# 320 dense tokens and 224 gathered slots in the expert stage, with all gate matrices made on TensorE

## The chip, the cores and the metric

The kernel runs on one core of one Trainium2 chip. The metric is the device time of one execution in microseconds (us); lower is better. The engines are TensorE (PE; its weight loads are listed as PEld), VectorE (DVE), ScalarE (ACT), GpSimd (POOL) and SyncE (SP). SP, ACT and POOL also issue DMAs.

## What is computed

One layer over 512 prompt tokens and 32 sample tokens, width 1024, all in float32. A mixer (gated attention with 8 heads of 64 beside a linear recurrence of width 512) is followed by a layer norm, and then by PEER, a retrieval over 16384 single-neuron experts:

```python
def peer_block(xb, w_query, keys_1, keys_2, u_tab, v_tab):
    qy = (xb @ w_query).reshape(n, 8, 2, 128)
    s1 = einsum("nhd,kd->nhk", qy[:, :, 0], keys_1)      # 128 keys per half
    s2 = einsum("nhd,kd->nhk", qy[:, :, 1], keys_2)
    t1, i1 = top_k(s1, 16); t2, i2 = top_k(s2, 16)
    cand = t1[..., :, None] + t2[..., None, :]           # 256 pairs
    top, sel = top_k(cand, 16); g = softmax(top)
    idx = take_along_axis(i1 * 128 + i2, sel)            # 8 heads x 16 experts of a token
    act = gelu(einsum("nhkd,nd->nhk", u_tab[idx], xb))
    return einsum("nhk,nhkd->nd", g * act, v_tab[idx])   # then residual and layer norm
```

## The kernel before

**Precision.** A float32 product is made of three TensorE passes: each operand is split into a rounded high part (a copy on ACT) and a low part (a subtraction), and `mm3` adds high*high, low*high and high*low. So every 128x1024 weight tile costs one DMA of 512 KB, one ACT copy and one subtraction (`split`, L112 to L119; `table` in the expert stage, L1146 to L1154). `pool_share` says which share of the subtractions of `split` goes to POOL; the others go to DVE.

**Stages.** `run` works in two groups of tokens: group 0 is the sample S (32) with prompt tiles P0 and P1 (128 each), group 1 is P2 and P3. The order is mixer(0), `out_first` (output projection, layer norm and PEER queries of group 0), mixer(1), `out_second` (the same for group 1), `experts`.

**Background.** Each `chunk` (24 matmuls over one weight tile) ends with `background`, which issues pieces from the list `bg` at a set rate (`MIX_RATE`, `OUT_RATE`). The pieces are zero fills of the gate matrix and the steps of `route`: for one head of one token tile, two rankings of 128 scores, a ranking of the candidate pairs, and the pick of indices and softmax weights (`gate`). The framework orders each engine's instructions by a modelled timeline, near the order in which they are issued; some are pinned by `keep_in_program_order`.

**Dense and gathered tokens.** For P0, P1 and P2 (384 tokens) all 16384 experts are computed in 128 blocks: `up(b)` (24 matmuls, 384 columns) and a GELU give a 128x384 activation tile, `down(b)` multiplies it with the gates of the block, splits it, and adds it into six PSUM banks with 18 matmuls of 512 columns. The first `down` follows 29 blocks behind `up` (`AHEAD`). For S (packed four times onto 128 partitions: 32 slots) and P3 (128 slots) the chosen rows alone are fetched: for each slot one indirect DMA on POOL's queue brings 128 rows of `peer_u` and another 128 rows of `peer_v` (512 KB each); DVE takes the dot product with h (`u_step`, L1068) and adds the weighted row (`v_step`, L1083). `RATE` gives the fetches per block; 29/10 per block is the usual one. Six buffers (`gat`) hold rows.

**Gates.** For P0 and P1 the gates are scattered into a zeroed matrix in DRAM by 256 indirect DMAs on POOL (`scatter`, L998, 16 per head and tile), each with an add; the 32 zero fills of 512 KB go through SP's queue. Every `down` reads its 128 KB of them (`gt`, L1172) behind all scatters. For P2 `gate_steps` builds 4 tokens at a time: DVE makes one-hot rows, TensorE multiplies them (L1041), ACT copies the result, and a DMA stores 16 tokens (`gatemat2`), which is read back in chunks of 16 blocks (`gg`, L1202).

**Queues near the change.** POOL's stream holds the scatters, the gathers, a memset of two rows of `qa` (L356) in mixer(1), and a share of the subtractions. SP's stream holds all weight loads in order and the two small DMAs of `forget` (L503, L504) into `ka` and `qa`, which attention needs.

## Time and profile before

| | us |
|---|---|
| median of 3 runs | 1828.71 (1826.39 to 1833.19) |
| the profiled execution | 1824.01 |
| its span, first to last instruction | 1822.2 |
| outside the span | 1.8 |
| busy PE, DVE, POOL, ACT | 1677.2, 1398.2, 928.0, 810.2 |
| DMA | 443.01 MB, mean 243 GB/s |

The profile is of one execution. A group of instructions is told by its line, engine and operands; "busy" is the union of its times, and "idle before" is how long its engine stood still just before, with what ended that. PE's instructions overlap, so the pace of matmuls is read from the chain of waits, where pieces follow each other without overlap.

### The profile page before, as it was taken

The numbers are of one execution on the slowest core, as the hardware profiler recorded it, in microseconds if no ns is written. First come the engines' busy times: TensorE is split into PE (matmuls) and PEld (weight loads), VectorE is DVE, ScalarE is ACT, GpSimd is POOL, SyncE is SP. The second block draws the span as 40 slices with busy tenths as digits, with TensorE's granted clock in tenths as the row PEclk, the third lists the DMA queues.
The fourth block names the chain that finished last, engine by engine and source line by source line (L and its number), as shares of the span: only waits on it lengthen the run. The fifth ranks groups of instructions, "written<-read, shape, count | busy, mean of one in ns | idle before, by whom it ended". The sixth has DMA issues, their size and how long they took to land.

```text
span 1822.2 us, 26970 instructions
## 1 busy us (share of the span) xinstructions
PE 1677.2 (92%) x9448; PEld 1511.8 (83%) x9448; DVE 1398.2 (77%) x3197; ACT 810.2 (44%) x1413; POOL 928.0 (51%) x623
## 2 busy tenths in 40 slices
PE   8999999994898999919999999999999999998896
PEld 7889889984687999918999899989999998997674
DVE  6634779884886789809998877877888878886877
ACT  7744455872645674503445333433333333332332
POOL 2110235888888888864443544453544445542340
PEclk9999999997899999959999999999999999999998
DMA  9863636673466656649989889998999888998883
GB/s 319 280 236 101 218 98 171 152 162 59 71 150 143 162 116 174 174 75 360 334 306 322 297 300 328 349 326 321 340 328 343 322 322 321 321 324 281 292 304 125
DMA packets 182201, 443.01 MB, mean 243 GB/s; under 512 B 53624, under 2 KB 80936, under 8 KB 181040
## 3 DMA queue, kind: packets, MB, share of 16 engines
q1 hardware_dynamic: 93568, 265.80, 42.8%
q0 software_dynamic: 82944, 167.94, 31.0%
q10 hardware_dynamic: 5552, 7.54, 1.3%
q8 instruction: 74, 1.21, 0.3%
q14 instruction: 63, 0.52, 0.1%
HBM read 409.80 MB, written 31.36 MB: 242 GB/s over the span
## 4 chain that ended last, share of the span: by engine, by line
PE 61%; DVE 8%; DMA 6%; POOL 5%; issue 3%; ACT 2%; SPq 0%; DVEq 0%; ACTq 0%; POOLq 0%
PE u L161 9%; PE u L164 9%; PE u L165 9%; PE y L164 8%; PE y L165 8%; PE y L161 8%; POOL gatemat L998 5%; PE mm L164 2%; PE mm L165 2%; PE mm L161 2%; DMA gat<-peer_v,idxP 2%; PE y L1041 1%; DMA vr<-peer_v 1%; DVE wl L119 1%; PE x L895 1%
## 5 line engine op out<-in xcount | busy, mean ns | idle before, releaser
L998 POOL DMA_INDIRECT gatemat<-gateP,idxP x256 | 441.8, 1726 | 94.8 <-issue 72.7
L165 PE MATMUL u<-hDh,ul 128*128 128x384 f32 x992 | 336.3, 339 | 41.3 <-DVE ul L1153 41.3
L161 PE MATMUL u<-hDh,uh 128*128 128x384 f32 x992 | 340.3, 343 | 5.9 <-DVE hS L1097 3.5
L164 PE MATMUL u<-hDl,uh 128*128 128x384 f32 x992 | 336.8, 340 | 0.0
L164 PE MATMUL y<-vl,pwh 128*128 128x512 f32 x768 | 303.1, 397 | 8.2 <-DVE vl L1153 8.1
L165 PE MATMUL y<-vh,pwl 128*128 128x512 f32 x768 | 301.8, 397 | 5.6 <-DVE pwl L1186 5.6
L1058 POOL DMA_INDIRECT gat<-peer_u,idxP x128 | 174.5, 1363 | 213.5 <-DVE ul L1153 43.5
L161 PE MATMUL y<-vh,pwh 128*128 128x512 f32 x768 | 276.5, 396 | 5.5 <-ACT vh L1152 5.5
L1058 POOL DMA_INDIRECT gat<-peer_v,idxP x128 | 172.0, 1344 | 210.0 <-DMA ur<-u_chunk 61.9
L1152 ACT CAST vh<-vr 128x1024 fp32r<-128x1024 f32 x128 | 134.2, 1050 | 296.4 <-DVE vl L1153 150.1
L165 PEld LDWEIGHTS u<-hDh,ul 128*128 128x128 f32 x992 | 188.0, 189 | 42.5 <-DVE ul L1153 42.5
L115 ACT CAST wh<-raw 128x1024 fp32r<-128x1024 f32 (+1 forms) x140 | 145.0, 1039 | 156.4 <-PE mm L164 123.4
L1083 DVE SCALAR_TENSOR_TENSOR accP<-gat,actP,accP 128x1024 f32<-128x1024 f32 x127 | 162.9, 1283 | 66.4 <-DMA gat<-peer_v,idxP 66.0
L119 DVE TENSOR_TENSOR wl<-raw,wh 128x1024 fp32r<-128x1024 f32 (+1 forms) x134 | 164.6, 1230 | 57.1 <-ACT wh L115 56.4
L1068 DVE SCALAR_TENSOR_TENSOR gat<-gat,hP 128x1024 f32<-128x1024 f32 x128 | 155.2, 1220 | 68.3 <-DMA gat<-peer_u,idxP 68.0
L161 PEld LDWEIGHTS u<-hDh,uh 128*128 128x128 f32 x992 | 188.2, 190 | 11.9 <-DVE hS L1097 4.4
L164 PEld LDWEIGHTS u<-hDl,uh 128*128 128x128 f32 x992 | 188.3, 190 | 4.2
L1152 ACT CAST uh<-ur 128x1024 fp32r<-128x1024 f32 x124 | 130.1, 1049 | 125.0 <-DMA ur<-u_chunk 56.9
L164 PEld LDWEIGHTS y<-vl,pwh 128*128 128x128 f32 x768 | 145.5, 189 | 42.8 <-DVE vl L1153 12.7
L165 PEld LDWEIGHTS y<-vh,pwl 128*128 128x128 f32 x768 | 145.4, 189 | 39.5 <-DVE pwl L1186 6.2
L161 PEld LDWEIGHTS y<-vh,pwh 128*128 128x128 f32 x768 | 144.8, 189 | 35.9 <-ACT vh L1152 7.3
L1153 DVE TENSOR_TENSOR vl<-vr,vh 128x1024 fp32r<-128x1024 f32 x128 | 155.9, 1218 | 15.7 <-ACT vh L1152 15.7
(367 smaller groups left out, 3438.1 us busy)
## 6 DMA issues: line engine op xcount, KB each, us to landing
vr<-peer_v SPq DMA_DIRECT2D x128, 512.0 KB
ur<-u_chunk SPq DMA_DIRECT2D x124, 512.0 KB
raw<-w_chunk SPq DMA_DIRECT2D x63, 512.0 KB
gatemat<-zero SPq DMA_DIRECT2D x32, 512.0 KB
raw<-w_q SPq DMA_DIRECT2D x32, 512.0 KB
gt<-gatemat SPq DMA_DIRECT2D x128, 128.0 KB
raw<-w_up SPq DMA_DIRECT2D x16, 512.0 KB
raw<-w_out SPq DMA_DIRECT2D x16, 512.0 KB
```

What stands on the lines that cost most here:

```text
L115: nc.scalar.copy(h, src)
L119: eng.tensor_tensor(out=l, in0=src, in1=h.bitcast(F32), op=OP.subtract)
L161: first = nc.tensor.matmul(out, lh, rh, start=start, stop=False)
L164: nc.tensor.matmul(out, lh, rl, start=False, stop=False)
L165: return first, nc.tensor.matmul(out, ll, rh, start=False, stop=stop)
L895: nc.tensor.matmul(ps[:, i], qT[:, t.col:t.col + t.n], self.keysT[:, half], start=True, stop=True)
L998: i = nc.gpsimd.indirect_dma_start(out=self.G, out_offset=bass.IndirectOffsetOnAxis(ap=t.idx[:, j:j + 1], axis=0), in_=t.gate[:, j:j + 1], ...
L1058: i = nc.gpsimd.indirect_dma_start(out=r, out_offset=None, in_=A[table], in_offset=bass.IndirectOffsetOnAxis(ap=t.idx[:, j:j + 1], axis=0))
L1068: nc.vector.scalar_tensor_tensor(out=r, in0=r, scalar=1.0, in1=t.h, op0=OP.mult, op1=OP.mult, accum_out=act[:, j:j + 1])
L1083: nc.vector.scalar_tensor_tensor(out=acc, in0=r, scalar=act[:, j:j + 1], in1=acc, op0=OP.mult, op1=OP.add)
L1152: nc.scalar.copy(h, raw)
L1153: nc.vector.tensor_tensor(out=l, in0=raw, in1=h.bitcast(F32), op=OP.subtract)
```

## The change

Of P0 only the second half (64 tokens) is still dense, so 320 tokens are dense (`ND`), and the first half (P0a: 64 tokens, packed twice, 64 slots) is gathered: 32 + 64 + 128 = 224 slots. One fetch of a slot brings a row of both tables (`peer_uv`, 8 KB per row, 1 MB per slot); three such buffers take the place of six of half the size. The 64 dense tokens of P0 use 2 products instead of 3 in `down`: low and high parts lie side by side in one 128-column weight, and a matmul with a selection matrix sums the two halves at the end.

All gates are built as those of P2 were; scatters, zero fills, `gt` and its wait are gone. The one-hot rows come from two DVE comparisons, the weighting from four ACT multiplications. `gg` is read in chunks of 8 blocks, issued 4 blocks ahead. Routing works on four heads at a time after the rankings. Nothing is routed in `out_first`; S, P0 and P1 are routed, the gates of P0 and P1 built, and the gathers of S (and whatever comes up of P0a) issued as background of mixer(1) (`early_rows`), four pieces per chunk. These early gathers have one row buffer, inside the tile that later holds h transposed (`hD`); `early_end` empties the list before that tile is filled, and h of group 0 goes through DRAM (`hN`).

In mixer(1) two of three `split` subtractions go to POOL, and in `experts` every `v` subtraction but the last four. The memset of `qa` moves to DVE, and four small DMAs of `forget` from SP's to ACT's queue. `AHEAD` is 32.

```diff
-POOL_SHARE = (1, 5), (0, 1)
-MIX_RATE = (6, 5), (3, 2)
+POOL_SHARE = (1, 5), (2, 3)
+MIX_RATE = (6, 5), (4, 1)
+MIX_GATHER = 3, 4
-OUT_RATE = (3, 2), (1, 1)
+OUT_RATE = (3, 2), (2, 1)
+HALF = 64
+ND = 384 - HALF
-         toks=[Tok("S", 0, 32), Tok("P0", 32, 128, 0, 0), Tok("P1", 160, 128, 128, 128)]),
+         toks=[Tok("S", 0, 32), Tok("P0", 32, 128, 0, 0, HALF), Tok("P1", 160, 128, 128 - HALF, 128)]),
-GT, GB = 16, 16
+GT, GB, UN, NB, LAG = 16, 8, 64, 4, 2
-AHEAD = 29
+AHEAD = 32
-NGAT = 6
+NGAT = 3
-GATHER = AHEAD
-RATE = (1, 1), (26, 10), (29, 10), (16, 10)
+GATHER = 27
+RATE = (1, 2), (13, 10), (16, 10), (8, 10)
...
-                (nc.vector if self.first else nc.gpsimd).memset(self.qa[DH:DH + 2], 1.0)
+                nc.vector.memset(self.qa[DH:DH + 2], 1.0)
...
-        nc.sync.dma_start(self.ka[DH:DH + 1, :, p0:p0 + npr], nF)
-        nc.sync.dma_start(self.qa[DH + 1:DH + 2, :, off:], F)
+        nc.scalar.dma_start(self.ka[DH:DH + 1, :, p0:p0 + npr], nF)
+        nc.scalar.dma_start(self.qa[DH + 1:DH + 2, :, off:], F)
...
+    def early_rows(self, toks):
+        nc, keep = self.nc, self.keep
+        S, P0, P1 = toks
+        ring = keep.tile([P, 2 * KD * max(ND, 288)], F32R, tag="hD", name="ring")
...
+        work = self.routing(S)
+        first = len(work)
+        work += self.routing(P0)
...
+            work.append(lambda: self.halve(P0, t))
+            gathered.append(t)
+        work += self.gate_steps(P0, vt, self.bank, nc.gpsimd, hots.append)
+        work += self.routing(P1)
+        work += self.gate_steps(P1, vt, self.bank, nc.gpsimd, hots.append)
+        for t in gathered:
+            self.steps += self.gather_steps(t)
+        self.bg += work[:first]
+        for i, w in enumerate(work[first:]):
+            self.bg.append(w)
+            if (i + 1) * MIX_GATHER[0] // MIX_GATHER[1] > i * MIX_GATHER[0] // MIX_GATHER[1]:
+                self.bg.append(self.early_step)
+        self.bg += [self.early_step] * 60
+
+    def early_step(self):
+        if self.steps and self.steps[0].tok.done:
+            parts = self.steps[0].parts
+            parts.pop(0)()
+            if not parts:
+                self.steps.pop(0)
+
+    def early_end(self):
+        for p in self.bg:
+            if p != self.early_step:
+                p()
+        self.bg = []
+        while self.steps[0].tok is self.early[0] or len(self.steps[0].parts) < 3:
+            self.early_step()
...
             self.project([t3], 1, lambda half, q: wo[q], behind=True)
+            self.early_end()
+            self.hDh, self.hDl = self.wide("hD")
+            for i, x in enumerate((self.hDh, self.hDl)):
+                nc.gpsimd.dma_start(x[:, :, :NDA], self.hN[:, i])
             self.turned([t2], pool, self.hDh[:, :, c], self.hDl[:, :, c])
...
         def make(t0):
...
+            for m, x in ((0, A), (1, B)):
+                nc.vector.tensor_tensor(out=x, in0=self.iotaK[:, None].to_broadcast(sh),
+                                        in1=T[:, m, t0:t0 + 4, None].to_broadcast(sh), op=OP.is_equal)
             for j in range(4):
+                nc.scalar.mul(A[:, j], A[:, j], T[:, 2, t0 + j:t0 + j + 1])
...
+        def fetch(j):
+            r = v[j] = self.row()
+            i = nc.gpsimd.indirect_dma_start(out=r.rearrange("p i d -> p (i d)"), out_offset=None, in_=A["peer_uv"],
                                              in_offset=bass.IndirectOffsetOnAxis(ap=t.idx[:, j:j + 1], axis=0))
         def u_step(j):
+            r, a = v[j], v["act"][:, j:j + 1]
+            nc.vector.scalar_tensor_tensor(out=r[:, 0], in0=r[:, 0], scalar=1.0, in1=t.h, op0=OP.mult, op1=OP.mult,
+                                           accum_out=a)
+            nc.scalar.activation(a, a, GELU)
+            nc.scalar.mul(a, a, t.gate[:, j:j + 1])
...
         def table(ap, name, stage=None):
...
-            nc.vector.tensor_tensor(out=l, in0=raw, in1=h.bitcast(F32), op=OP.subtract)
+            eng = nc.gpsimd if name == "v" and not stage else nc.vector
+            eng.tensor_tensor(out=l, in0=raw, in1=h.bitcast(F32), op=OP.subtract)
...
         def down(b):
-            gt = pool.tile([P, NS], F32, tag="gt", name="gt", bufs=3)
-            i = nc.sync.dma_start(gt, gates[b * P:(b + 1) * P])
-            for s in [i for c in self.scatters.values() for i in c]:
-                tc.add_manual_dep(i.ins, s.ins.name, SYNC, reason="all heads are in")
-            nc.vector.tensor_tensor(out=a[:, :NS], in0=a[:, :NS], in1=gt, op=OP.mult)
-            a2 = a[:, NS:].rearrange("p (q t) -> p q t", t=GT)
-            nc.vector.tensor_tensor(out=a2, in0=a2, in1=gg[b // GB][:, :, b % GB], op=OP.mult)
+            a3 = a.rearrange("p (q t) -> p q t", t=GT)
+            nc.vector.tensor_tensor(out=a3, in0=a3, in1=gg[b // GB][:, :, b % GB], op=OP.mult)
+            pw = pool.tile([P, UN + 2 * ND], F32R, tag="pw", name="pw", bufs=LAST)
...
+                    if t.nd == UN:
+                        first = nc.tensor.matmul(o, pw[:, :P], vh[:, cs], start=start, stop=False)
+                        nc.tensor.matmul(o, pw[:, :P], vl[:, cs], start=False, stop=stop)
+                    else:
+                        first, _ = self.mm3(o, ph[:, ts], pl[:, ts], vh[:, cs], vl[:, cs], start, stop)
```

## Rows read from the trace of the kernel before

**Rows 1.** Busy time by stage: engine busy us (instructions), clock, DMA share, GB/s.
```profile
core 0: us, PE busy (x) PEld busy (x) DVE busy (x) ACT busy (x) POOL busy (x), PEclk, DMA share, GB/s
0.00:262.00 262.00, 246.21 (x1596) 219.58 (x1597) 154.05 (x336) 143.53 (x249) 42.99 (x44) 0.97 0.65 215
...
322.00:537.00 215.00, 176.68 (x1260) 159.34 (x1259) 166.40 (x630) 130.15 (x279) 183.40 (x106) 0.90 0.56 114
537.00:637.00 100.00, 92.08 (x634) 86.87 (x632) 70.18 (x202) 56.52 (x123) 85.06 (x50) 0.97 0.68 162
637.00:823.00 186.00, 145.23 (x890) 143.53 (x891) 128.47 (x442) 84.84 (x149) 148.25 (x89) 0.88 0.59 138
823.00:1637.00 814.00, 807.96 (x4029) 730.30 (x4028) 685.12 (x1138) 310.89 (x449) 376.79 (x275) 1.00 0.91 326
1637.00:1822.20 185.20, 150.41 (x627) 118.23 (x626) 139.82 (x247) 51.67 (x74) 53.87 (x43) 0.94 0.72 250
```
**Rows 2.** PE's waits from 322 to 823 us: total, times, longest.
```profile
PE u L165 <- DVE ul L1153: 38.8, 2, 38.2
PE x L588 <- DMA ka<-z: 30.2, 1, 30.2
```
**Rows 3.** Chain of waits, 440 to 462 us: start, us, what.
```profile
453.35 1.81 POOL qa L356
```
**Rows 4.** Chain of waits: matmuls of the gates and of the dense blocks.
```profile
695.85 3.57 PE y L1041 x32
...
833.05 1.40 PE y L161 x6
...
841.44 1.40 PE y L161 x6
```
**Rows 5.** DVE groups of the dense stage, 1033 to 1637 us: busy, mean ns, idle before.
```profile
L1068 DVE SCALAR_TENSOR_TENSOR gat<-gat,hP 128x1024 f32<-128x1024 f32 x108 | 131.0, 1220 | 59.6 <-DMA gat<-peer_u,idxP 59.3
L1083 DVE SCALAR_TENSOR_TENSOR accP<-gat,actP,accP 128x1024 f32<-128x1024 f32 x99 | 127.0, 1283 | 47.0 <-DMA gat<-peer_v,idxP 46.8
...
L1153 DVE TENSOR_TENSOR ul<-ur,uh 128x1024 fp32r<-128x1024 f32 x71 | 86.4, 1216 | 0.0
L1186 DVE TENSOR_TENSOR pwl<-acts,pwh 128x384 fp32r<-128x384 f32 x71 | 39.1, 550 | 0.0
```
**Rows 6.** DVE groups of routing (322 to 537 us) and of the gates (from 637 us).
```profile
L977 DVE TENSOR_REDUCE ii<-oh 128x16 f32<-128x512 bf16 x13 | 8.8, 674 | 0.0
...
L915 DVE MAX8 tv<-sc 128x8 f32<-128x128 f32 x20 | 5.1, 277 | 0.0
...
L1033 DVE TENSOR_TENSOR hot<-iotaK,pairT 128x512 f32<-128x512 f32 x32 | 21.9, 686 | 1.4 <-ACT pairT L1023 1.2 <-PE y L1041 0.2
```
**Rows 7.** Timelines, DVE and POOL beside each other: start, us, instruction.
```profile
185.52 2.41 POOL L119 TENSOR_TENSOR wl<-raw,wh 128x1024 fp32r<-128x1024 f32 x1 [28.18 <-ACT wh L115]
...
185.76 2.48 DVE L668 SCALAR_TENSOR_TENSOR mTl<-sg,mTh 128x288 fp32r<-128x288 f32 x1 [0.15 <-ACT mTh L667]
...
188.72 0.46 DVE L668 SCALAR_TENSOR_TENSOR mTl<-sg,mTh 128x288 fp32r<-128x288 f32 x1
...
254.62 9.63 DVE L795 TENSOR_TENSOR hDl<-hT,hDh 128x288 fp32r<-128x288 f32 x4
256.22 5.17 POOL L800 TENSOR_TENSOR hP<-hP,g 128x1024 f32<-128x1024 f32 x2
```
**Rows 8.** POOL groups of the whole span.
```profile
L1058 POOL DMA_INDIRECT gat<-peer_u,idxP x128 | 174.5, 1363 | 213.5 <-DVE ul L1153 43.5 <-DMA ur<-u_chunk 40.1 <-issue 32.5
...
L119 POOL TENSOR_TENSOR wl<-raw,wh 128x1024 fp32r<-128x1024 f32 x6 | 14.4, 2404 | 107.7 <-ACT wh L115 90.3 <-DVE nm L593 17.4
```
**Rows 9.** Busy time of one stretch of the dense stage (columns as in rows 1).
```profile
1100.00:1200.00 100.00, 100.00 (x501) 90.57 (x501) 82.52 (x115) 35.02 (x50) 43.94 (x33) 1.00 0.94 340
```
**Rows 10.** ACT groups: table loads (262 to 637 us) and gate copies (637 to 823 us).
```profile
L409 ACT ACT_TABLE_LOAD x4 | 5.1, 1283 | 0.1
...
L1043 ACT COPY stage<-y 128x512 f32<-128x512 f32 x32 | 18.2, 588 | 8.9 <-PE y L1041 8.7
```

More of the change, by code (lines that the diff above doesn't have):

```diff
@@ L989, in route @@
-        return [lambda: rank(0), lambda: rank(1), pair, pick]
-    def scatter(self, t, h):
-        tc, nc = self.tc, self.nc
-        before = self.scatters.get(t, self.zeroing)
-        cur = []
-        for j in range(h * TOPK, (h + 1) * TOPK):
-            i = nc.gpsimd.indirect_dma_start(out=self.G, out_offset=bass.IndirectOffsetOnAxis(ap=t.idx[:, j:j + 1], axis=0),
-                                             in_=t.gate[:, j:j + 1], in_offset=None, compute_op=OP.add)
-            tc.declare_no_dep(i.ins, group="gate", keep=[b.ins for b in before],
-                              reason="distinct cells, or ordered by hand")
-            for b in before:
-                tc.add_manual_dep(i.ins, b.ins.name, SYNC, reason="same cell in two heads")
-            tc.add_to_no_dep_group("gate", i.ins)
-            cur.append(i)
-        self.scatters[t] = cur
@@ L1015, in gate_steps @@
+        return ([lambda i=i, half=half: rank(i, half) for i in range(nb) for half in range(2)] + [pair] +
+                [lambda i=i: choose(i) for i in range(nb)] + [pick, take])
+    def gate_steps(self, t, tile_, psum, queue, free=lambda x: None):
         nc = self.nc
@@ new lines, in multiply, with step @@
+            ps = ps.rearrange("p (t i) -> p i t", i=NK)
+            for m, st in enumerate(v["stage"]):
+                r = slice(m * NK // 2, (m + 1) * NK // 2)
+                nc.scalar.copy(st[:, :, c:c + 4], ps[:, r])
+                if c + 4 == GT:
+                    dst = self.G[(t.dense + i) // GT].rearrange("p (i t) -> p i t", t=GT)
+                    queue.dma_start(dst[:, r], st)
+        def step(t0):
+            if todo and (t0 is None or len(todo) >= LAG):
+                todo.pop(0)()
+            if t0 is not None:
+                make(t0)
@@ L1086, in gather_steps, with step @@
+            if j == t.ns - 1:
+                self.gathered(t, acc)
+        def step(j):
+            if j == 0:
+                self.flush()
+                begin()
+            fetch(j)
+            u_step(j)
+            self.flush()
+            self.pending = lambda: v_step(j)
         steps = []
-        for g0 in range(0, t.ns, G):
-            steps += [lambda j=j: u_step(j) for j in range(g0, g0 + G)]
-            steps += [lambda j=j: v_step(j) for j in range(g0, g0 + G)]
-        steps.append(lambda: fin(t, v["acc"]))
```

436 lines of the change are left out of this document (244 added, 192 removed).

## The prediction

> **What bounds the kernel now.** I read the stages first [rows 1]. In the dense stage (823 to 1637 us) PE is busy 808 of 814 us, DVE 685, DMA at a share of 0.91: PE sets the time, the others follow closely. Ahead of it PE loses its time in two places [rows 2]: 30.2 us in mixer(1), where attention waits for `ka`, whose DMA waits for the memset that runs on POOL behind the scatters [rows 3], and 38.2 us before the first `down`, which waits for all scatters. The last 185 us belong to nobody: PE 150, DVE 140, DMA at 0.72. So time can be had from the matmuls, from the two waits, and from the end. The question to put to each stage is which engine is second.
>
> **Prices.** Six `y` matmuls take 1.40 us, so one is 0.233, and a block comes every 8.39 us [rows 4]; 18 are 4.20, so 24 `u` matmuls of 384 columns are 4.19, or 0.175 each. By these two points 320 columns cost 0.146. On DVE an instruction starts about 0.08 us before its predecessor's recorded end, so 1.22 and 1.28 us in rows 5 occupy 1.14 and 1.20. A gathered slot, both products and the read of the accumulator, is then 2.44 us of DVE, a low part 1.14, a gate comparison 0.60 [rows 6]. Routing one head is 36 instructions, from a ranking (277 ns) to the reduction (674 ns), about 8.0 us recorded and 5.8 occupied [rows 6]; for four heads together the rankings stay, the small steps are shared, and I get 5.1 per head.
>
> **0 to 322 us.** The 32 zero fills leave SP's queue; PE is idle for 16 us in the first 262 [rows 1], mostly before its first weights. Nothing else there changes but routing, which was beside a full PE. I take -3 (0 to -8).
>
> **322 to 537 us, mixer(1): +100.** Both causes of the 30.2 us wait go: the scatters, and the memset's place behind them. The two DMAs of `forget` now stand in ACT's queue, behind its activations. Next comes DVE. 50 chunks at four pieces issue 200 of the listed pieces here, 24 more in `out_second`. DVE now: 166 us, of which 13 heads of routing are 75, so 91 is its own. The change takes 27 subtractions to POOL (-31) and adds the memset (+2): 62. It adds routing for 18 head tiles (92), 48 gate steps of two comparisons (58), and 33 early slots (81); 20 of this falls in the next stage. Sum 62 + 92 + 58 + 81 - 20 = 273 us, against 215 for the whole stage now, and PE's 177 + 48 x 0.89 = 220. So DVE sets this stage, by at least 60 us more than now. ACT is close behind: 130 now, a GELU per early slot between Exp and Tanh costs two table loads of 1.28 us [rows 10], some 24 times (62 us), and the gates' copies and multiplications about 1.2 x 48 = 58: 250. ACT is the next bound, not the first.
>
> The 27 subtractions on POOL take 2.40 us each [rows 8] and are not free for DVE: while POOL's L119 ran from 185.52 to 187.93, a DVE instruction that takes 0.46 alone took 2.48 and ended 0.3 after it, and four such took 9.63 beside L800 [rows 7]. A DVE instruction with two SBUF operands stands still while POOL runs one. 65 us of POOL work cost DVE between 0 and 65; I take 25. Early slots have one row buffer, so a dot product follows its fetch by one piece of work while 1 MB must land; DVE stands for some of that. 298 us at 95% is 315: +100, from +60 (DVE without a gap) to +175.
>
> **537 to 637 us: +10.** PE 92 of 100. DVE loses half of P2's routing to later and gains 20 us; h of group 0 must come back from DRAM into the tile that the early gathers leave, through POOL's queue, and PE's next products wait for it. 0 to +25.
>
> **637 to 823 us: -53.** The 38.2 us wait goes. PE: 28 blocks of 24 x 0.146 = 3.50, and 32 gate steps of 0.89: 127. DVE: 28 low parts 32, P2's routing 20, gates 38, P3's routing 19, three slots 7: 116. Next is the first read of `gg` on SP's queue, which waits for the last gate store with the `u` loads behind it: 6 us. 133, so -53 (-60 to -40).
>
> **823 to 1637 us, the dense stage: -12.** A block needs of PE 3.50 + 16 x 0.233 = 7.22 us, 1.17 less than now. For 1.6 slots per block DVE needs 1.14 + 0.40 (gates at 320 columns, scaled from L1186 [rows 5]) + 0.40 (low part) + 1.6 x 2.44 = 5.84. That would hide; but all of these have two SBUF operands, and POOL's `v` subtraction of 2.40 shuts them out. Together 8.24 us per block. On DVE this subtraction cost 1.14; on POOL it costs DVE twice that. The Trainium skill, "SBUF — State Buffer", section "SBUF: two separate sides", says that the shared port pair is an exclusive lock held for the whole instruction; by it the block is 8.2, without it 7.2 by PE, and rows 7 agree with the lock. DMA: 1 MB of tables, 1.68 MB of rows and 0.16 of gates are 2.89 MB per block; at the 340 GB/s that the trace held without a PE wait [rows 9] this is 8.5 us, but no row shows the limit, and larger packets may help: 7.6 to 8.9. I take 8.35 from the port, where DVE's own waits for rows (59.6 + 47.0 us in 604 [rows 5]) are partly hidden by POOL's. The first 16 blocks also carry P3's routing, at fewer slots. 96 blocks x 8.35 = 802 instead of 814. Bounds: 7.6 (-84) to 8.9 (+40).
>
> **From 1637 us: +55.** 28 blocks have `y` alone: PE 3.73, but DVE 0.80 + 0.8 x 2.44 and POOL 2.40 on one port, 5.2: 146 us, where 25 blocks took 124. By the counts of `RATE` 3 + 149 + 22 = 174 slots are issued by then; of 96 early-type slots 34 are done before, so 190 - 174 = 16 are left, at 2.6 us (2.44 of DVE, 1 MB of DMA): 42. The end after the last row is 61 now, 9 of it gathers that are counted above: 52. 240 instead of 185. Bounds +15 to +90.
>
> **Sum.** -3 + 100 + 10 - 53 - 12 + 55 = +97 us. On the profiled execution 1824.0 + 97 = 1921; that execution lies 4.7 us under the median, so 1926 is my forecast for the median.
>
> **Rivals.**
> 1. Port not decisive (faster). If POOL and DVE interleave better than rows 7, blocks come at DMA's 7.6 (-84), mixer(1) at DVE's floor (+60), the end at 28 x 4.5 + 80 (+21), the rest at its best (0, -60, -5): -68, 1761. It turns faster when a block is under 7.3 us with all else as forecast, or under 7.9 with mixer(1) at its floor. For it: no POOL subtraction stands in the dense stage now. Against: rows 7.
> 2. DMA sets the blocks. 8.9 us in the dense stage (+40) and +90 at the end: 1828.7 + 184 = 2013. For it: the share of 0.91 now [rows 1], and and 2.89 MB per 7.22 us of PE are a quarter more than 326 GB/s x 8.39 us = 2.74 MB per 8.39; against: packets of 8 KB instead of 4 KB. The Trainium skill, "DMA: Bandwidth & Descriptors", section "Bandwidth", gives 425 GB/s for a 16 MB load; as an estimate from that page a block's DMA would take 6.8 us and this rival would fall away. No row here holds such a rate over a stage.
> 3. Mixer(1) packs fully: +60 there, 1886. Against: early slots with one buffer.
> 4. The change does not do what it says of "early" and "background": DVE stands for each fetch (some 4 us x 33) and mixer(1) costs +200: 2026.
>
> **How the numbers follow.** Forecast 0.58 (1860 to 1990); rival 1 0.13, rival 2 0.12, rival 3 0.10, rival 4 0.07. The range 1810 to 2030 leaves out most of rival 1 and the tails. A measurement of this kernel can tell about 0.5% from no change: faster 0.14 (rival 1 and a little of rival 3), same 0.06, slower 0.80.
>
> **What would show it.** Right: DVE over 90% busy in mixer(1) and that stage over 290 us; no L998; `v` subtractions on POOL with 2.4 us, DVE products beside them at 2.5 to 3.6 instead of 1.2; PE under 90% busy in the dense stage at 8.2 to 8.5 us per block; some 16 slots after the last `u` blocks with PE idle. Wrong: DVE products at 1.22 throughout; blocks at 7.2 to 7.6; mixer(1) near 215; the first `y` well before 860 us (forecast: 319 + 315 + 110 + 133 = 877).

## The result and the profile after

The changed kernel takes 2203.0 us in the median (2197.5 to 2209.1), the kernel before beside it 1831.0 us: a ratio of 1.204, with an interval of 1.199 to 1.208. Forecast were 1926 us and a range of 1810 to 2030. The direction was right, the size was not, and the time lies 173 us outside the range.

Busy time by stage of the changed kernel, in the stages of [rows 1] (columns as there):

```profile
0.00:326.00 326.00, 305.14 (x2021) 273.05 (x2021) 176.93 (x351) 169.37 (x308) 52.22 (x44) 0.98 0.49 154
326.00:745.00 419.00, 264.14 (x1680) 234.93 (x1678) 326.11 (x832) 256.46 (x623) 131.06 (x82) 0.80 0.47 160
745.00:892.00 147.00, 85.07 (x603) 78.53 (x601) 84.21 (x206) 56.35 (x129) 12.36 (x13) 0.79 0.51 161
892.00:1057.00 165.00, 142.35 (x956) 139.05 (x957) 138.72 (x349) 107.13 (x284) 11.85 (x6) 0.91 0.65 209
1057.00:1931.00 874.00, 747.28 (x3801) 656.83 (x3801) 716.09 (x858) 355.98 (x806) 469.81 (x242) 0.94 0.86 308
1931.00:2196.00 265.00, 143.19 (x537) 100.75 (x535) 192.00 (x256) 72.80 (x184) 115.50 (x66) 0.84 0.65 229
```

Set against the forecast:

| stage | before | forecast | after | missed by |
|---|---|---|---|---|
| to the end of `out_first` | 322 | 319 | 326 | +7 |
| mixer(1) | 215 | 315 | 419 | +104 |
| out_second | 100 | 110 | 147 | +37 |
| `u` alone | 186 | 133 | 165 | +32 |
| dense stage | 814 | 802 | 874 | +72 |
| end | 185 | 240 | 265 | +25 |

In no stage behind 326 us is an engine busy for 90% of the time: every one is longer than the work of its busiest engine. PEclk is the granted clock of TensorE; behind 326 us it is 0.79 to 0.94, where the kernel before had 0.88 to 1.00 [rows 1]. In mixer(1) PE is busy 264 of 419 us and DVE 326. What PE stands for between 322 and 1057 us (PE's instruction, what it waits for: total us, times, longest), to be laid beside [rows 2]:

```profile
PE x L1092 <- DVE pairP L1067: 95.7, 3, 69.3
PE x L1200 <- DVE accS L1169: 37.1, 1, 37.1
PE x L1118 <- ACT ring L1108: 20.4, 18, 6.5
PE mm L165 <- DMA hD<-hnorm: 19.4, 1, 19.4
PE u L169 <- DVE ul L1271: 18.7, 6, 6.8
```

The first line is the transpose that opens the gate steps: it needs the routing's results. The second is the selection matmul that sums S's four partial rows after its last early slot; `early_end` forces it before `hD` is filled. All of it is background work, and PE takes it in order, with the mixer's own products queued behind.

The dense stage: DVE's products and, on the last line, POOL's `v` subtraction, 1057 to 1931 us (busy us, mean ns, idle before and its cause). The DVE lines answer to [rows 5] (1220 and 1283 ns), the POOL line to the 2404 ns of [rows 8]:

```profile
L1169 DVE SCALAR_TENSOR_TENSOR accP<-gat,actP,accP 128x1024 f32<-128x1024 f32 x87 | 148.7, 1709 | 16.5 <-ACT actP L1162 16.5
L1159 DVE SCALAR_TENSOR_TENSOR gat<-gat,hP 128x1024 f32<-128x1024 f32 x89 | 131.7, 1480 | 30.1 <-DMA gat<-peer_uv,idxP 30.1
L1298 DVE TENSOR_TENSOR pw<-acts,pw 128x320 fp32r<-128x320 f32 x95 | 76.3, 803 | 11.7 <-ACT pw L1297 11.6
...
L1271 POOL TENSOR_TENSOR vl<-vr,vh 128x1024 fp32r<-128x1024 f32 x93 | 265.6, 2856 | 192.8 <-ACT vh L1269 192.4
```

These means mix two kinds of instructions. Of the 87 sums on the first line 48 ran while POOL was subtracting and took 2.06 us on the mean, the other 39 took 1.28 as before; the `u` subtraction of DVE, which seldom met one of POOL's (6 times in 95), kept 1.22 us. One meeting in the timeline (start, us, engine, instruction, idle before):

```profile
1503.07 1.28 DVE L1169 SCALAR_TENSOR_TENSOR accP<-gat,actP,accP 128x1024 f32<-128x1024 f32 x1
1504.47 3.29 POOL L1271 TENSOR_TENSOR vl<-vr,vh 128x1024 fp32r<-128x1024 f32 x1 [3.17 <-ACT vh L1269]
...
1506.09 2.74 DVE L1169 SCALAR_TENSOR_TENSOR accP<-gat,actP,accP 128x1024 f32<-128x1024 f32 x1 [0.60 <-ACT actP L1162]
```

The end, from 1931 us, has one stand of PE that no row of before had:

```profile
PE y L1312 <- ACT vh L1269: 54.2, 1, 54.2
```

It is the time of the slots that are left over: the last four blocks stage their `v` tiles in the row buffers (`gat`, three of them), which these slots hold. PE stands from 2104 to 2158 us, and 16 slots run from 2102 to 2158.

### The profile page after: what moved, and what is told of

Its sections match the earlier page's. It is cut to its first block, busy times and chain, and to the rows that moved or that the text cites. A ratio compares the mean times of both kernels' runs of the same rounds, so it can differ in the third digit from the quotient of the medians.

```text
span 2195.7 us, 27335 instructions
## 1 busy us (share of the span) xinstructions
PE 1687.2 (77%) x9590; PEld 1483.1 (68%) x9590; DVE 1634.1 (74%) x2849; ACT 1018.1 (46%) x2331; POOL 792.8 (36%) x451
## 5 line engine op out<-in xcount | busy, mean ns | idle before, releaser
L1271 POOL TENSOR_TENSOR vl<-vr,vh 128x1024 fp32r<-128x1024 f32 x124 | 340.2, 2744 | 337.2 <-ACT vh L1269 225.5
L169 PE MATMUL u<-hD,ul 128*128 128x320 f32 x992 | 337.9, 341 | 92.7 <-DVE ul L1271 92.4
L165 PE MATMUL u<-hD,uh 128*128 128x320 f32 x992 | 331.4, 334 | 57.2 <-ACT uh L1269 54.7
L168 PE MATMUL u<-hD,uh 128*128 128x320 f32 x992 | 327.3, 330 | 0.0
L169 PEld LDWEIGHTS u<-hD,ul 128*128 128x128 f32 x992 | 204.1, 206 | 115.9 <-DVE ul L1271 115.5
L165 PEld LDWEIGHTS u<-hD,uh 128*128 128x128 f32 x992 | 204.9, 207 | 68.5 <-ACT uh L1269 62.0
L1151 POOL DMA_INDIRECT gat<-peer_uv,idxP x128 | 174.2, 1361 | 156.2 <-DVE accP L1169 84.1
L168 PE MATMUL y<-vl,pw 128*128 128x512 f32 x512 | 205.7, 402 | 18.3 <-POOL vl L1271 18.3
L165 PE MATMUL y<-vh,pw 128*128 128x512 f32 x512 | 190.5, 403 | 29.4 <-ACT vh L1269 29.3
L168 PEld LDWEIGHTS u<-hD,uh 128*128 128x128 f32 x992 | 204.5, 206 | 3.0
L169 PE MATMUL y<-vh,pw 128*128 128x512 f32 x512 | 201.6, 394 | 0.0
L1271 DVE TENSOR_TENSOR ul<-ur,uh 128x1024 fp32r<-128x1024 f32 x124 | 153.4, 1237 | 58.4 <-ACT uh L1269 58.4
L1298 DVE TENSOR_TENSOR pw<-acts,pw 128x320 fp32r<-128x320 f32 x128 | 115.9, 906 | 41.4 <-ACT pw L1297 41.2
L1312 PE MATMUL y<-vh,pw 128*128 128x512 f32 x256 | 95.8, 395 | 54.2 <-ACT vh L1269 54.2
```

What stands on the lines that cost most here:

```text
L165: first = nc.tensor.matmul(out, lh, rh, start=start, stop=False)
L168: nc.tensor.matmul(out, lh, rl, start=False, stop=False)
L169: return first, nc.tensor.matmul(out, ll, rh, start=False, stop=stop)
L1151: i = nc.gpsimd.indirect_dma_start(out=r.rearrange("p i d -> p (i d)"), out_offset=None, in_=A["peer_uv"], in_offset=bass.IndirectOffsetOn ...
L1271: eng.tensor_tensor(out=l, in0=raw, in1=h.bitcast(F32), op=OP.subtract)
L1298: nc.vector.tensor_tensor(out=pl, in0=a, in1=ph.bitcast(F32), op=OP.subtract)
```

## The experiments

The theories after this comparison: (A) the shared port of DVE and POOL makes the dense stage; (B) DMA makes it; and for mixer(1): (C) PE stands in order at the transposes; (D) POOL's subtractions hold the weights back; (E) the early slots over one row buffer are a serial chain.

### The dense stage

**v subtraction back on DVE.**

```diff
-            eng = nc.gpsimd if name == "v" and not stage else nc.vector
+            eng = nc.vector
```

> The changed kernel with one thing undone: the v subtraction of every down goes back from POOL to DVE. Stage to look at: dense stage, 874 us for 96 blocks = 9.1 us per block, DVE products 1.79 (v_step) and 1.40 (u_step). Theory port lock: without a POOL subtraction the products return to 1.28 and 1.22, a block needs 1.14 + 1.14 + 0.80 + 1.6 x 2.44 = 7.0 of DVE and 7.2 of PE, so the block falls to 7.4 to 8.0 us, the dense stage by 105 to 160 and the end by 20 to 40: total 2000 to 2080. Rival DMA (2.89 MB per block): the block stays at 8.6 to 9.1 and the total above 2140, with the DMA share unchanged near 0.86. Rival ACT in order (its slot GELU waits 251 us for dot products in this stage): products get short but the block stays above 8.4.

Measured: 2082.5 us, ratio 1.138 (1.133 to 1.143), 120 us less than the changed kernel and just above the upper end of the port theory; the stage gave 94 us where 105 were the least expected. Its stages from the first `y` on, one 100 us stretch of the dense stage, and its DVE products there:

```profile
1054.00:1834.00 780.00, 721.16 (x3802) 640.65 (x3801) 674.74 (x956) 358.37 (x806) 207.41 (x149) 0.96 0.94 345
1834.00:2081.00 247.00, 137.30 (x536) 103.73 (x535) 173.83 (x284) 73.10 (x183) 48.38 (x37) 0.82 0.69 244
...
1400.00:1500.00 100.00, 94.10 (x498) 83.44 (x497) 87.26 (x113) 45.81 (x105) 25.65 (x20) 0.97 0.97 365
```
```profile
L1169 DVE SCALAR_TENSOR_TENSOR accP<-gat,actP,accP 128x1024 f32<-128x1024 f32 x88 | 112.6, 1279 | 0.0
L1159 DVE SCALAR_TENSOR_TENSOR gat<-gat,hP 128x1024 f32<-128x1024 f32 x89 | 108.6, 1220 | 10.1 <-DMA gat<-peer_uv,idxP 10.1
```

The products are back at 1279 and 1220 ns although DVE now does these subtractions too, and a block takes 780 / 96 = 8.1 us instead of 9.1: 94 us less in the stage and 18 at the end. The edit also takes the subtractions out of POOL's queue, where fetches stand behind them, so this alone does not name the port. The two traces do. In the changed kernel DVE or a subtraction of POOL runs for 771 of the 874 us, and neither for 103; here DVE runs for 676 of the 780 us, and stands for 104. The standing is the same; what went is 95 us of work that could not run side by side. So the port costs 1.0 us per block. The block doesn't reach PE's 7.2, however, and DMA now has a share of 0.94 at 345 GB/s.

**Half of each row fetch.** The same kernel, with rows of 4 KB in the expert stage:

```diff
-            i = nc.gpsimd.indirect_dma_start(out=r.rearrange("p i d -> p (i d)"), out_offset=None, in_=A["peer_uv"],
-                                             in_offset=bass.IndirectOffsetOnAxis(ap=t.idx[:, j:j + 1], axis=0))
+            half = not self.early_on
+            i = nc.gpsimd.indirect_dma_start(out=r[:, 0] if half else r.rearrange("p i d -> p (i d)"), out_offset=None,
+                                             in_=A["peer_v" if half else "peer_uv"], in_offset=bass.IndirectOffsetOnAxis(ap=t.idx[:, j:j + 1], axis=0))
...
+            r = r if self.early_on else r[:, 0:1].to_broadcast([P, 2, D])
```

> The kernel with the v subtraction on DVE (2082.5), and each fetch of the expert stage brings one row of 4 KB in place of 8 KB; both DVE products of a slot read that row (so the gathered tokens' rows are not the reference's). A block moves 2.05 MB in place of 2.89, all engine work stays. There the dense stage ran at 8.1 us per block, 345 GB/s at a share of 0.94, with PE busy 721 of 780 us. Theory DMA: the block falls to 7.4 to 7.7 us, the dense stage by 40 to 65, the end by 10 to 25: total 2000 to 2030. Rival, the chain ACT to DVE to PE of the tables sets 8.1: total 2065 to 2085.

Measured: 1996.3 us, ratio 1.091 (1.087 to 1.094), 86 us less than the run above and a little under the range of the DMA theory. Its stages, and the one long wait of PE in the first of them:

```profile
1050.00:1786.00 736.00, 693.70 (x3803) 624.16 (x3802) 666.68 (x969) 374.13 (x809) 232.89 (x147) 0.97 0.77 261
1786.00:1991.00 205.00, 131.02 (x537) 100.89 (x535) 172.85 (x288) 74.81 (x185) 49.56 (x38) 0.84 0.59 194
```
```profile
PE u L1203 <- DVE accP0a L1172: 34.5, 1, 34.5
```

A block takes 736 / 96 = 7.7 us with the same engine work. So behind the port stand the bytes of the rows, worth 44 us here and 42 at the end; whether by the rate of DMA or by the earlier landing of each row, this run does not separate. Of the 1.9 us between PE's 7.2 and the measured 9.1 the port makes 1.0 and the bytes 0.46. The rest, 0.46 or 44 us, is in this run for the greater part the one wait above: PE comes to the matmul that sums P0a's rows before DVE has them (0.3 us in the run above). The Trainium skill, "DMA: Bandwidth & Descriptors", section "Bandwidth", gives 425 GB/s for a 16 MB load; this mix of tables, rows and gates ran at 345 GB/s over 780 us and at 365 in its best stretch shown, with a share of 0.94 to 0.97. The measurement decides: at 365 GB/s a block of 2.89 MB takes 7.9 us, and no 100 us of the dense stage of any run here moved more than 366 GB/s.

### Mixer(1) and out_second

**No weight subtractions on POOL (D).**

```diff
-POOL_SHARE = (1, 5), (2, 3)
+POOL_SHARE = (1, 5), (0, 1)
```

> The changed kernel with no weight subtraction on POOL in mixer(1) (share 2 of 3 before). mixer(1) takes 419 us in the changed kernel, 215 in the one before. Theory DVE and the gate transposes: DVE gets 27 x 1.14 = 31 us more and is spared 25 us of lock, the PE waits at the transposes of the gate steps (95.7 us) stay: mixer(1) 400 to 450, total within 30 of 2203. Rival POOL in order: its subtractions stand behind row fetches that wait for the one row buffer (118 us), and weight loads wait for them (226 us on SP's queue), so without them mixer(1) falls by 60 to 120 us, total 2080 to 2150.

Measured: 2215.3 us, ratio 1.213 (1.209 to 1.218): nothing won, 12 us lost. In the changed kernel SP's queue stands 226 us for POOL's `wl`, but the loads behind it are not what PE waits for.

**Gate steps behind all routing (C).**

```diff
-        work += self.gate_steps(P0, vt, self.bank, nc.gpsimd, hots.append)
         work += self.routing(P1)
+        work += self.gate_steps(P0, vt, self.bank, nc.gpsimd, hots.append)
         work += self.gate_steps(P1, vt, self.bank, nc.gpsimd, hots.append)
```

> The changed kernel with the background of mixer(1) in another order: routing of S, P0 and P1 first, then the gate steps of P0 and P1 (in the changed kernel the gate steps of P0 stand between the routings of P0 and P1). Same work. Theory PE in order: PE stands 69.3 + 26.4 us at the first transposes of P0's and P1's gates because the routing that feeds them is late on DVE, and the products of the mixer stand behind them; with both routings ahead only one such wait can be left and it comes later, so the stage falls by 40 to 80 us towards DVE's 326 us of work: total 2120 to 2165. Rival DVE occupancy: DVE has the same 326 us of work and 43 us of fetch waits, PE then waits for low parts of weights instead; total 2185 to 2210.

Measured: 2204.7 us, ratio 1.207 (1.203 to 1.212), no change. PE's waits from 326 to 897 us:

```profile
PE x L1200 <- DVE accS L1169: 81.9, 1, 81.9
PE x L1092 <- DVE pairP L1067: 53.4, 3, 34.0
```

The transposes give 42 us back and S's selection matmul takes 45. Here the chain of the slots lies bare. The timeline of 19 us of that wait (start, us, engine, instruction, idle before):

```profile
766.40 1.22 DVE L1159 SCALAR_TENSOR_TENSOR ring<-ring,hS 128x1024 f32<-128x1024 f32 x1 [5.95 <-DMA ring<-peer_uv,idxS]
...
767.67 0.20 ACT L1161 ACTIVATE actS<-actS 128x1 f32<-128x1 f32 x1 [8.54 <-DVE ring L1159]
767.91 0.29 ACT L1162 ACTIVATE actS<-actS,gateS 128x1 f32<-128x1 f32 x1
768.23 1.28 DVE L1169 SCALAR_TENSOR_TENSOR accS<-ring,actS,accS 128x1024 f32<-128x1024 f32 x1 [0.60 <-ACT actS L1162]
769.79 0.94 POOL L1151 DMA_INDIRECT ring<-peer_uv,idxS  x1 [8.13 <-DVE accS L1169]
775.59 1.23 DVE L1159 SCALAR_TENSOR_TENSOR ring<-ring,hS 128x1024 f32<-128x1024 f32 x1 [6.07 <-DMA ring<-peer_uv,idxS]
```

From one dot product to the next 9.2 us pass: 1.2 for the product, 0.5 for ACT's two small steps, 1.3 for the sum, 0.3 and 0.94 for POOL to issue the next fetch, 4.9 until it has landed (770.73 to 775.59). No two of them overlap. In the changed kernel S's 32 dot products run from 381.8 to 788.8 us, 13.1 us apart on the mean and 8.9 at the least.

**Transposes that wait for nothing (C again).**

```diff
+                src = self.ident if psum == self.bank else src
                 nc.tensor.transpose(ps[:, i * P:(i + 1) * P], src, self.ident)
```

> The changed kernel, but the transposes that open the gate steps of P0 and P1 read a constant tile in place of the routing's results (the gates of P0's second half and of P1 come out wrong; the amount of work is the same). PE then never waits for the routing at these transposes (95.7 us in the changed kernel), all else stays. Theory PE in order: mixer(1) and out_second together fall from 566 us by 50 to 95, total 2110 to 2155. Rival DVE chain: the same 410 us of DVE work and 65 us of fetch waits must be done before S's sums are there, so PE waits instead at S's selection matmul (37.1 us now) or for low parts, and the total is 2185 to 2210, as it was with the gate steps moved (2204.7).

Measured: 2194.1 us, ratio 1.200 (1.197 to 1.202). The wait at the transposes is gone, PE ends the last product of the output projection at 654 us instead of 755, and then stands at the selection matmul:

```profile
PE x L1201 <- DVE accS L1170: 127.5, 1, 127.5
```

So (C) falls as the bound of this kernel: while the slots are late, PE's order decides only where it stands, not until when. S's sums are ready at 782 to 797 us in the changed kernel and in both of these.

**No early fetches, and no early slots (E).** In the first only the first fetch is made, in the second 2 of S's 32 slots remain:

```diff
+        self.early_on = True
...
+            if self.early_on and j:
+                return
             i = nc.gpsimd.indirect_dma_start(out=r.rearrange("p i d -> p (i d)"), out_offset=None, in_=A["peer_uv"],
```
```diff
-            self.steps += self.gather_steps(t)
+            g = self.gather_steps(t)
+            self.steps += [g[0], g[-1]] if t is S else g
...
-        if self.steps and self.steps[0].tok.done:
+        if self.steps[0].tok is self.early[0] and self.steps[0].tok.done:
...
-        while self.steps[0].tok is self.early[0] or len(self.steps[0].parts) < 3:
+        while self.steps[0].tok is self.early[0]:
```

> The changed kernel with the early row fetches left out but the first (the DVE, ACT and PE work of the early slots is done on that one row; the output is not the reference's in the rows of S and of the first half of P0). Theory one row buffer: DVE's waits for rows (42.9 us in mixer(1), 22.3 in out_second), POOL's waits for the free buffer (118 us) and what stands behind them in POOL's and SP's queues go: mixer(1) and out_second together fall from 566 us by 60 to 110: total 2090 to 2140. Rival: fetches are hidden behind the other late work of DVE: at most 25 us less, 2178 to 2203.

> The changed kernel with 2 of the 32 sample slots (30 left out, so S's rows are not the reference's) and none of P0a's early; fetches, DVE products, GELUs of these slots are all gone from mixer(1) and out_second. Leaving out the fetches alone gave 77 us. Theory DVE occupancy: the DVE work of 30 slots, 30 x 2.44 = 73 us, comes on top: total 2045 to 2075 (with 5 us back for P0a's two slots in the dense stage). Rival, only the fetch waits count, the DVE work of the slots is hidden: 2115 to 2135.

Measured: 2126.4 us, ratio 1.165 (1.160 to 1.169), and 2062.7 us, ratio 1.128 (1.125 to 1.130). The waiting for rows is worth 77 us, and the DVE work of 30 slots (30 x 2.44 = 73) another 64: nearly all of it is on the path. In the first, PE stands 112 us at the first transposes while DVE is busy 109 of them, with slots and P0's routing in a row:

```profile
397.00:509.00 112.00, 0.20 (x2) 0.00 (x0) 109.14 (x284) 35.64 (x97) 3.54 (x4) 0.51 0.04 13
```

Mixer(1) and out_second of both runs (two rows each), and PE's longest wait in the second run:

```profile
327.00:736.00 409.00, 256.18 (x1727) 227.99 (x1725) 348.42 (x871) 249.45 (x632) 92.07 (x59) 0.82 0.32 106
736.00:820.00 84.00, 72.64 (x562) 71.29 (x560) 61.04 (x168) 50.43 (x108) 4.22 (x3) 0.93 0.54 164
...
326.00:668.00 342.00, 256.49 (x1741) 227.39 (x1741) 270.64 (x783) 227.75 (x564) 90.47 (x62) 0.90 0.40 132
668.00:745.00 77.00, 71.11 (x560) 70.11 (x558) 58.54 (x159) 48.66 (x107) 2.39 (x1) 0.98 0.48 158
```
```profile
PE x L1093 <- DVE pairP L1068: 52.7, 3, 44.4
```

The two stages take 566 us in the changed kernel, 493 without the fetches and 419 with 2 slots. DVE stands for 156, 84 and 90 us of them. So the fetches make 72 us of DVE's standing, and more than half of it is there without them.

**Gate steps in the expert stage.**

```diff
-BUILD = 5, 2
+BUILD = 5, 1
...
-ROUTE = (2, 1), (1, 1)
+ROUTE = (4, 1), (1, 1)
...
-        work += self.gate_steps(P0, vt, self.bank, nc.gpsimd, hots.append)
         work += self.routing(P1)
-        work += self.gate_steps(P1, vt, self.bank, nc.gpsimd, hots.append)
...
-        build = self.gate_steps(dense[-1], built, gbank, nc.sync)
+        build = [s for t in dense for s in self.gate_steps(t, built, gbank, nc.sync)]
```

> The changed kernel with the gate steps of P0 and P1 built in the expert stage beside the u products, ahead of P2's (5 steps per block in place of 2.5), so that mixer(1) holds routing and early slots only. Theory: mixer(1) loses 48 steps of PE (48 x 0.89 = 43 us), 58 of DVE and the 95.7 us in which PE stands for routing; DVE then still has about 350 us of work in mixer(1) and out_second: these fall from 566 to 450 to 490; the stage of u alone, 165 us now, has 89 steps of about 1.2 on DVE and 0.89 on PE beside 28 u blocks: 210 to 240. Total 2130 to 2180. Rival, the early slots' chain sets mixer(1) (S's selection matmul waits): mixer(1) and out_second stay above 530 and the total rises to 2220 or more.

Measured: 2240.1 us, ratio 1.224 (1.221 to 1.227), the rival's result. All of P0's and P1's gate work is out of mixer(1), and mixer(1) with out_second still takes 862 - 326 = 536 us. Its 166 us from 580 on, and PE's wait in them:

```profile
580.00:746.00 166.00, 0.00 (x0) 0.00 (x0) 62.34 (x112) 16.48 (x55) 16.89 (x18) 0.50 0.32 114
```
```profile
PE x L1198 <- DVE accS L1167: 185.8, 1, 185.8
```

PE does nothing, DVE is busy for 62 of 166 us, POOL for 17, DMA has a share of 0.32. No engine and no queue sets this stretch; the latency of one slot does, at 8.8 us each.

**Two row buffers.** In the changed kernel the second buffer has to come out of the same tile, from the one-hot rows of the gate steps (three to one):

```diff
-        row = part(3, 2).rearrange("p (i d) -> p i d", i=2)
-        hots = [part(i, 1) for i in range(3)]
-        self.row = lambda: row
+        rows = [part(i, 2).rearrange("p (i d) -> p i d", i=2) for i in (1, 3)]
+        hots = [part(0, 1)]
+        self.row = lambda: rows.append(rows.pop(0)) or rows[-1]
...
+        lag = 1 if psum == self.bank else LAG
```

> The changed kernel with two row buffers for the early slots in place of one, in the same tile (one buffer of one-hot rows in place of three, so the products of a gate step follow its comparisons at once); the fetch of a slot is issued ahead of the dot product of the slot before it. With one buffer a slot is a chain of 9.0 us where nothing else runs (dot product 1.22, GELU and weight 0.5, sum 1.28, issue 0.94 and 0.25, landing 4.9) and 32 of them fill 382 to 789 us. Theory chain: with two buffers a slot comes every 4.5 to 7 us, S is done before the last gate step, the 37.1 us at S's selection matmul go and the order of the rest is DVE's: total 2110 to 2150, near the run without fetches (2126). Rival DVE order: the slots are late because the pieces of routing and gates stand between them on DVE: above 2175.

Measured: 2225.4 us, ratio 1.215 (1.211 to 1.219), a miss of both theories: S is done at 602 us instead of 792, but the gate steps now end at 822 instead of 744, since comparisons and products wait for each other. DVE's wait for PE, 322 to 900 us:

```profile
DVE ring L1106 <- PE x L1119: 68.0, 35, 2.2
```

The chain is shorter, and the tile's space, not DVE, paid for it. So the test was made where the tile is free, in the kernel with the gate steps in the expert stage; it differs from that kernel by the buffer, and the fetch one slot ahead that goes with it, alone:

> The kernel with P0's and P1's gate steps in the expert stage (2240.1), now with two early row buffers in the same tile; nothing else differs. Theory chain: a slot comes every 4.5 to 7 us in place of 11.2, S's sums are there by 540 to 620 us in place of 746, and the 185.8 us that PE stands at S's selection matmul shrink to under 40: mixer(1) and out_second 380 to 430 us in place of 537, total 2080 to 2140. Rival DVE order: slots still end after 700 us and the total is above 2190.

Measured: 2126.0 us, ratio 1.161 (1.157 to 1.164), 114 us less. Slots come every 7.5 us instead of 11.5 (4.5 to 7 were expected), S's sums are there at 621 us instead of 746, and PE's wait has shrunk:

```profile
326.00:623.00 297.00, 212.37 (x1247) 182.12 (x1246) 270.24 (x743) 198.05 (x364) 108.40 (x67) 0.77 0.58 204
623.00:736.00 113.00, 101.53 (x682) 93.08 (x681) 87.72 (x213) 61.82 (x134) 8.09 (x7) 0.95 0.54 174
```
```profile
PE x L1199 <- DVE accS L1168: 33.9, 1, 33.9
```

Mixer(1) and out_second take 410 us, and DVE is at 91% up to 623 us: the chain has given way to DVE's work, the bound that the prediction had named. (E) holds, with DVE's occupancy close behind. The second buffer gave 114 us here and nothing beside the gate steps, from whose space it was taken (2225.4 us), so how much each of the two is worth depends on the other.

**Both repairs.** The `v` subtraction on DVE with each of the two kernels with two buffers:

> The changed kernel with both repairs: two early row buffers, and the v subtraction on DVE. If the two causes are independent (one in mixer(1), one in the dense stage), this is the sum of both: 120 us less than the run with two buffers, 1990 to 2030. If the time won early is given back in the dense stage (the rows fetched there collide with more transfers), above 2050.

> The same with the v subtraction on DVE too. If the causes add up, 110 to 130 us less than the kernel with two buffers and the gate steps in the expert stage: 1960 to 2020. If DMA, at 345 GB/s in the dense stage after that repair, takes part of it back: less than 90 us less.

Measured: 2096.6 us, ratio 1.146 (1.142 to 1.150), and 1982.9 us, ratio 1.082 (1.079 to 1.085): 129 and 143 us less than the same kernels without it, where the `v` subtraction alone gave 120. The causes in the dense stage and in mixer(1) add up; nothing is given back. The first total lies outside the expected range only because the run with two buffers, from which it counts, did.

### The kernel before

**The memset of `qa` on DVE, nothing else.**

```diff
-                (nc.vector if self.first else nc.gpsimd).memset(self.qa[DH:DH + 2], 1.0)
+                nc.vector.memset(self.qa[DH:DH + 2], 1.0)
```

> The kernel before with one thing of the change alone: the memset of two rows of qa goes from POOL, where it stands behind scatters, to DVE. The DMA into ka that attention waited 30.2 us for stands in SP's queue behind weight loads and before the DMA into qa that waits for the memset. Theory: the wait goes and DVE has room there, 1828 falls to 1798 to 1810. Rival: the DMAs stand behind weight loads on SP anyway, or the time comes back at the 38.2 us wait for the scatters ahead of the first down, which start and end when they did: 1820 to 1830.

Measured: 1831.1 us, ratio 1.002 (1.000 to 1.003). The 30.2 us of [rows 2] are gone, and the 38.2 have become 73.9. PE's wait before the first `down`, and POOL's scatters from 300 to 823 us:

```profile
PE u L165 <- DVE ul L1153: 77.4, 3, 73.9
...
L998 POOL DMA_INDIRECT gatemat<-gateP,idxP x250 | 435.5, 1742 | 76.2 <-issue 71.6 <-DMA gatemat<-gateP,idxP 0.9 <-ACT sc L901 0.3
```

250 scatters in 435.5 + 76.2 us: one every 2.05 us, back to back. The two waits of PE were one chain, that of POOL, and it ends when it ends.

**Half of the scatters.** P1's gates built on TensorE like P2's, only P0's scattered:

```diff
-NS = 256
-GT, GB = 16, 16
+NS = 128
+GT, GB = 16, 8
-BUILD = 5, 2
+BUILD = 4, 1
-ROUTE = (2, 1), (1, 1)
+ROUTE = (3, 1), (1, 1)
```

> The kernel before, with the memset on DVE and half of what the change does to the gates: only P0's gates are scattered (128 scatters), P1's are built on TensorE as P2's are, in the stage of u alone (4 steps per block in place of 2.5). POOL issued the 256 scatters back to back at 2.0 us from 295 to 820 us, and with the memset moved PE stood 73.9 us ahead of the first down for the last of them. Theory: the scatters end before 620 us, the first down waits for its u blocks and gate steps only (from 605 us, 28 x 4.19 + 65 x 0.89 = 175 on PE): first y at 780 to 800 in place of 821 to 824, total 1785 to 1810. Rival: DVE (28 low parts, P2's routing, 64 gate steps of 1.8) sets the stage: 190 to 220 us, first y at 800 to 825, total 1815 to 1835.

Measured: 1809.2 us, ratio 0.987 (0.984 to 0.990), at the slow end of the theory: 1.3% less than the kernel before. The stage of `u` alone, between the end of the queries and the first `y`:

```profile
611.00:800.00 189.00, 176.89 (x1167) 172.80 (x1165) 174.36 (x564) 102.84 (x178) 4.90 (x5) 1.00 0.53 182
```

The scatters end at 576 us, POOL is out of the way, and PE is busy for 177 of 189 us, with DVE, the rival, at 174.

## Why the prediction was wrong

**Mixer(1), +100 forecast, +204 measured: the step that failed.** The prediction priced the early slots by what they occupy on DVE, 33 x 2.44 = 81 us, said that DVE "stands for some" of the landing, and put all standing of DVE at 5% of the stage, 17 us. With one buffer the next fetch can't start before the product of the last row is done, so the slots are a chain, and its length is a price of its own. Rows of before give a lower bound: the two products of [rows 5], and 1 MB at the 340 GB/s of [rows 9], 3.1 us, are 5.6 us per slot, 33 x 5.6 = 185 us. That bound alone would still have fitted into the 315 us of the forecast. In the changed kernel a slot is 8.9 us at least, since a row lands 4.9 us after its issue and POOL's and ACT's small steps come on top: 285 us for S, which can't start before S is routed (382 us) and so can't end before 667; with DVE's other pieces between it ended at 792. And `hD` ties this end to the path: the early rows lie in the tile that the expert stage's h needs.

In the stage's own numbers: DVE was to be busy 298 us, the lock included, and to stand for 17. It was busy 326 and stood 93. The 28 us of work, each instruction taken from its predecessor's recorded end: routing 102 (forecast 92), gate comparisons 62 (58), slots 66 (61), the mixer's own work with its subtractions and the lock 96 (62 and 25). So the terms of work were each right within 11 us, and three quarters of the stage's miss are the 76 us of standing that the 5% left out.

Not all of this standing is the chain. The fetches are worth 77 us of the total, and half or a little more of the 141 us that mixer(1) and out_second missed together. With 2 slots the two stages still take 419 us, where the forecast without the price of the slots is 425 - 81 / 0.95 = 340. There PE is busy for 328 us, 16 more than forecast for the two stages, and stands 53 at the transposes, and DVE stands 90 us. That the gate steps, which PE takes in order, make this is likely: with them out of mixer(1) and two buffers DVE stands for 52. But no run took the gate steps and the slots out together, so how this part of the miss divides stays open.

**out_second, +10 forecast, +47 measured.** S's selection matmul (37.1 us) was not seen, the return of h into `hD` (19.4 us) was, as "0 to +25".

**`u` alone, -53 forecast, -21 measured.** Up to 1020 us the blocks came as worked out (3.5 us apart, 5.3 to 6 with gate steps). The low parts of the last three came 9 to 16 us apart: DVE, busy 41 of the 46 us from 1011 on, had 32 multiplications with `gg` (L1293, 14.8 us), P3's first rankings and three slots between them. The rankings and the slots were in this stage's sum; the multiplications were counted to the next.

**Dense stage, -12 forecast, +60 measured.** The mechanism was right, and its sum too: DVE and POOL's subtractions on one port were to take 8.24 us per block, and the time in which one of them runs is 771 / 96 = 8.03. The term that failed is the standing beside it. It was put at 0.11 us (8.35 in all, DVE's own waits "partly hidden by POOL's") and was 103 / 96 = 1.07. Port and DMA were set against each other as rivals, of which one decides; in the runs they add, 9.1, 8.1 and 7.7 us per block with both, with DMA alone, and with less of that. PE's terms held at the full clock: 24 `u` matmuls of 320 columns run 0.145 us apart (0.146). But after its stands PE ran at the lower of its two levels, 1.2 GHz, where they start 0.27 us apart; 271 steps of this stage are such, 33 us that the sum had at nothing. In the run with the `v` subtraction on DVE they are 139, in that with half rows 26. How much of them lies on the path was not measured.

**End, +55 forecast, +80 measured.** The 28 blocks of `y` alone took 6.1 us (5.2 forecast) and the 16 slots 3.5 us (2.6); what is left was some 14 us shorter. The blocks were priced too low by the same two causes as in the dense stage: they take 5.5 us without the port and 4.2 with half rows too. The slots were not. PE's stand for them, 54.2 us, stays without POOL's subtractions and nearly so with half of the bytes (the two runs in this order):

```profile
PE y L1312 <- ACT vh L1269: 53.8, 1, 53.8
...
PE y L1315 <- ACT vh L1272: 50.6, 1, 50.6
```

So neither port nor bytes price a slot there. The chain of a slot over three buffers, 8.9 / 3 = 3.0 us, comes near it; this is an estimate from the slots in mixer(1) and not shown.

**Rivals.** Rival 4 ("DVE stands for each fetch") had the size of mixer(1), +200, and nearly the mechanism, and got 0.07; its size is in part luck, since it priced the fetches at 4 x 33 = 132 us and they are worth 77. It left all other stages as forecast and so came to 2026. Rival 2 (DMA sets the blocks, 8.9 us and +90 at the end) lies nearer to the measured 9.1 us and +80 than the forecast does, by luck: with the port out of the way DMA's block is 8.1 us. As the second cause it is confirmed. Rivals 1 and 3 fell. The range was built from one stage's bounds at a time, but all six misses had one sign, and five of the six stages lie outside their own bounds. The 7 us of the first stage were not looked into.

**Sums.** Two of the prediction's sums are a little off: 298 us at 95% are 314, and with mixer(1) at its floor the time turns faster under 7.8 us per block, not 7.9. Nothing hung on either.

**What was to show it.** Right: a mixer(1) over 290 us, PE under 90% in the dense stage, the 16 slots, no L998. Wrong: DVE over 90% busy in mixer(1) (78%), blocks of 8.2 to 8.5 us (9.1), the first `y` at 877 us (1057), `v` subtractions of 2.4 us (2.86), DVE products of 2.5 to 3.6 us beside them (1.48 and 1.71 on the mean; 2.06 for the sums that met one).

**The two waits of before.** The prediction took 30.2 and 38.2 us as two sums to be had. They were one chain on POOL, and removing the first alone moved nothing. In the changed kernel both went with the scatters, so this did not spoil the forecast.

## What to carry to other kernels

Work put "in the background" has two prices, what it occupies and how long its chain is; with one buffer the chain is the number of steps times the whole latency of a step, and if its end is tied to the path (by a tile that is needed next, or a matmul that an in-order engine has queued), the chain is the price. Before a wait is counted as a gain, look for the chain behind it: if the same queue ends the next wait too, only shortening that queue helps. An engine that shares a port is no spare engine: count both sides' instructions as one sequence, at the durations that they have alone (side by side each one's record holds its wait for the other), and give the standing beside that sum a price of its own.

## What was not expected of the hardware

- With POOL subtracting 128x1024 tiles beside DVE's products, both sides stretch: on the mean of the stage POOL from 2.40 to 2.86 us, DVE's accumulation from 1.28 to 1.71, its 320-column subtraction from 0.49 to 0.80. Without POOL's, DVE's products are at 1.28 and 1.22 again in the same stage. The Trainium skill, "SBUF — State Buffer", section "SBUF: two separate sides", calls the pair an exclusive lock held for a whole instruction. The trace agrees: at the durations alone DVE's work is 676 - 114 = 562 us and POOL's 93 x 2.40 = 223, in all 785, and the time in which one of them runs is 771.
- An indirect fetch of 128 rows of 8 KB, alone on its queue, lands 4.9 us after POOL's instruction for it ends: 1.05 MB in 4.86 us are 216 GB/s, where the same DMA engines hold 345 GB/s over a stage.
- Scatters with an add leave POOL one every 2.05 us when nothing else holds them back (256 from 288 to 811 us in the kernel with the memset moved).
- TensorE pays for its stands a second time: the granted clock is 0.5 in the stands of mixer(1) (0.50 over the 166 us shown above), and after stands in the dense stage a `u` matmul of 320 columns starts every 0.27 us instead of 0.146, until the clock is granted in full again.
